# One value product for the high and the low part of the probabilities, in an attention and convolution block

## The chip, the cores and the metric

The kernel runs on one core of a Trainium2 chip. The metric is the device time of one execution in microseconds (us); less is better. The kernel before takes 1517.45 us, the median of three runs (1516.55 to 1518.78).

## The reference

One layer of a streaming encoder on x of 2048 tokens by 1024 features, in float32:

```
h    = rmsnorm(x, norm_g)
q, k, v, z_att, B, C, u, z_conv, g_att, g_conv = split(h @ w_in)
att  = chunked attention(q, k, v), 8 heads of 64, chunks of 64 tokens,
       each sees its own chunk and the 8 before, with a bias by clipped distance
A    = (att * silu(z_att)) @ w_att_out
Bc   = (B * conv3_causal(C * u) * silu(z_conv)) @ w_conv_out
m    = sigmoid(g_att) * A + sigmoid(g_conv) * Bc
out  = rmsnorm(x + m @ w_out, final_norm_g)
```

Inside the attention, per head, the softmax of the scores gives the probabilities p, and the value product is p times v over a band of 576 keys.

## The kernel before

**Number format.** Matrix products are made in a rounded float32 format. To keep float32 accuracy an operand is split into a high part (rounded) and a low part (the rest). A product of two split operands takes three passes (high by high, high by low, low by high; `passes`, lines 137 to 142).

**Stages.** The two halves of the sequence (1024 tokens each) go through the input projection one after the other; the columns of w_in are taken in 24 pairs of tiles, each pair in seven products (a two by two scheme with seven instead of eight). Operands that are used again lie in DRAM (q, k, v, z, gates, weights), and are loaded back. During the second half's projection the attention runs interleaved with it: `attention` is a generator, and the loop over the projection's products calls it so that it comes to its end with them (one step after about every product). Last come the output projections (`half_c`, `half_d`).

**Attention.** The sequence is cut into 4 chunks c of 512 tokens (columns), each with 8 heads h; a chunk and head has 4 units g of 128 queries. Each step of the generator handles three units in different states: the value product of a pair of units, three steps behind (`att_v`, line 223, called for every second unit); the transposes of a unit two steps behind (`att_t`, line 210); the scores of the newest unit (`att_s`, line 186).

- `att_s`: score products into the two-bank tile ps_s (line 195; the tile has one buffer), then VectorE adds the bias and finds the maximum (line 201), ScalarE takes the exponential with the row sum (205), VectorE the reciprocal (206), ScalarE scales (207). The result pr has three buffers.
- `att_t`: TensorE transposes up to five 128x128 blocks of pr into the two-bank tile ps_t (215; one buffer). ScalarE copies them to the high part (220), VectorE writes the rest to the low part (221). High and low part are two tiles, pth and ptl, of 6 key blocks by 256 queries (two units), one buffer each.
- `att_v`: for a pair of units (g0 = 0 or 2) TensorE sums over six key blocks j of 128 keys (line 233). The left operand vv holds, for 128 keys, the high part of v in 64 columns and the low part in 64 others, so the 128 rows of the result are p by v-high and p by v-low. Four blocks are seen by both units (256 columns); block 0 by the first unit alone and block 5 by the second alone (128 columns each). Each block has two matmuls, one with pth and one with ptl, that add up in the same columns. In the first chunk only keys from the sequence's beginning on exist: the spans are fewer.
- Both calls of a head fill one PSUM bank (512 columns, the tile po from a pool of one buffer). After the second call ScalarE copies rows 64 to 127 out (239) and VectorE adds rows 0 to 63 to them (240), into the tile o of a pair of heads (64 rows for each head). After the odd head the pair is multiplied with silu(z) (242), split in high (243) and low (244), and both are stored (246) by DMAs that POOL issues. The tiles zs and o have one buffer each, and so has vv; they are allocated when v of the head is loaded (`load_v`, line 172).

**PSUM.** During the attention: two banks for ps_s, two for ps_t, one for po, three for the projection (ps_d).

**Order of the work.** Except in the first stage, the order in which each engine's queue is filled is not written by hand: a planner in the framework takes the program's order as priority and its own estimate of when each operand is ready, and assigns buffers of a pool as they become free. The engines then work their queues in order. The temporary of the readout (line 238) comes from a pool of eight 128x512 buffers (tag e) that the projection's evictions use as well.

Of the kernel before, what the change touches and what calls it, by code (L numbers as in the profile page):

```python
# [17 lines left out]
P = 128  # L18
# [8 lines left out]
DH = 64  # L27
# [14 lines left out]
def block_kernel(ctx, tc, xb, xt, wp_in, wy, wo, bias, ng, fg, cw, cb, out):  # L42
    nc = tc.nc
# [62 lines left out]
    e = lambda name: ep.tile([P, CH], F32, tag="e", name=name)  # L106
    bank = lambda name: ps_m.tile([P, CH], F32, tag="m", name=name)
# [37 lines left out]
    def attention(ab):  # L145

        at = lambda shape, tag, dt=F32R, bufs=1: ab.tile(shape, dt, tag=tag, name=tag, bufs=bufs)
        pt = [at([P, 6, 2 * P], f"pt{s}") for s in "hl"]
        heads = {}
        values = {}  # L150
        pair = {}
        po = {}
        dma = nc.gpsimd.dma_start

        def load_qk(c, h):
            o = slice(h % 2 * DH, h % 2 * DH + DH)
            q = [at([P, CH], f"q{s}", bufs=2) for s in range(2)]
            kk = at([P, 2 * CH], "kk", bufs=2)
            bs = at([P, WIN], "bs", F32, bufs=2)
            heads[c, h] = (q, kk, bs)  # L160
            for s in range(2):
                for r in (0, DH):
                    dma(q[s][r:r + DH, :].bitcast(F32), q_d[h // 2][s][c][o, :])  # L163
            if c % 2:
                dma(kk.bitcast(F32), k_d[h][c // 2])
            else:
                dma(kk[:, CH:].bitcast(F32), k_d[h][c // 2][:, :CH])
                if c:
                    dma(kk[:, :CH].bitcast(F32), k_d[h][c // 2 - 1][:, CH:])
            dma(bs, bias_d[h])  # L170

        def load_v(c, h):
            vv = at([P, 8, P], "vv")
            values[c, h] = vv
            if c % 2:
                dma(vv.bitcast(F32), v_d[h][c // 2])
            else:
                dma(vv[:, 4:, :].bitcast(F32), v_d[h][c // 2][:, :4, :])
                if c:
                    dma(vv[:, :4, :].bitcast(F32), v_d[h][c // 2 - 1][:, 4:, :])  # L180
            if h % 2 == 0:
                zs = at([P, CH], "zs", F32)
                dma(zs, z_d[h // 2][c])
                pair[c, h // 2] = (zs, at([P, CH], "o", F32))

        def att_s(c, h, g):
            q, kk, bs = heads[c, h]
            nb = 5 if c else g + 1
            n = nb * P
            k1 = CH + (g + 1) * P  # L190
            ps = ps_s.tile([P, 2, CH], F32, tag="s", name="ps_s")
            parts = [(0, n)] if nb < 5 else [(0, WIN // 2), (1, WIN // 2)]
            for i, m in parts:
                for s in range(2):
                    nc.tensor.matmul(ps[:, i, :m], lhsT=q[s][:, g * P:(g + 1) * P], rhs=kk[:, k1 - n + i * m:k1 - n + (i + 1) * m], start=(s == 0), stop=(s == 1))  # L195
            if nb < 5:
                view, bv = ps[:, 0, :n], bs[:, WIN - n:]
            else:
                view, bv = ps[:, :, :WIN // 2], bs.rearrange("p (i m) -> p i m", i=2)
            nmax = small.tile([P, 1], F32, tag="nmax", name="nmax")  # L200
            nc.vector.tensor_tensor_reduce(out=view, in0=view, in1=bv, scale=-0.125, scalar=3.0e38, op0=ALU.add, op1=ALU.min, accum_out=nmax)  # L201
            pr = at([P, WIN], "pr", F32, 3)
            rs = small.tile([P, 1], F32, tag="rs", name="rs")
            out = pr[:, :n] if nb < 5 else pr.rearrange("p (i m) -> p i m", i=2)
            nc.scalar.activation(out, view, AF.Exp, bias=nmax, scale=-1.0, accum_out=rs)  # L205
            nc.vector.reciprocal(rs, rs)  # L206
            nc.scalar.activation(pr[:, :n], pr[:, :n], AF.Identity, scale=rs)  # L207
            return pr, nb

        def att_t(g, pr, nb):  # L210
            hi, lo = pt
            n = nb * P
            ps = ps_t.tile([P, 2 * CH], F32, tag="t", name="ps_t")
            for j in range(nb):
                nc.tensor.transpose(out=ps[:, j * P:(j + 1) * P], in_=pr[:, j * P:(j + 1) * P], identity=ident)  # L215
            o = g % 2
            js = slice(5 - nb + o, 5 + o)
            qs = slice(o * P, (o + 1) * P)
            src = ps[:, :n].rearrange("p (j q) -> p j q", q=P)
            nc.scalar.copy(hi[:, js, qs], src)  # L220
            nc.vector.tensor_sub(lo[:, js, qs], src, hi[:, js, qs].bitcast(F32))  # L221

        def att_v(c, h, g0):

            vv = values[c, h]
            if g0 == 0:
                po[0] = bank("po")
            ps = po[0]
            spans = [(4, 0, 2), (3, 0, 2), (2, 0, 2), (1, 0, 2), (0, 0, 1), (5, 1, 2)]
            js = [s for s in spans if c or g0 + s[0] >= 4]  # L230
            for i, (j, a, b) in enumerate(js):
                for s in pt:
                    nc.tensor.matmul(ps[:, (g0 + a) * P:(g0 + b) * P], lhsT=vv[:, g0 + j, :], rhs=s[:, j, a * P:b * P], start=(i == 0 and s is pt[0]), stop=(i == len(js) - 1 and s is pt[1]))  # L233
            if g0 == 0:
                return
            rows = slice(h % 2 * DH, (h % 2 + 1) * DH)
            zs, o = pair[c, h // 2]
            tmp = e("ot")
            nc.scalar.copy(tmp[rows], ps[DH:P])
            nc.vector.tensor_add(o[rows], ps[0:DH], tmp[rows])  # L240
            if h % 2:
                nc.vector.tensor_mul(o, o, zs)
                nc.scalar.copy(zs.bitcast(F32R), o)
                nc.vector.tensor_sub(o.bitcast(F32R), o, zs)
                for s, t in enumerate((zs, o)):
                    dma(mid_d[0][h // 2][s][c], t)

        todo = [(c, h) for c in range(NC) for h in range(HEADS)]
        units = [(c, h, g) for c, h in todo for g in range(4)]
        held = {}  # L250
        load_qk(*todo[0])
        for i in range(len(units) + BACK):
            u = i - BACK
            if u >= 0 and u % 2:
                att_v(*units[u][:2], units[u][2] - 1)
            if 1 < i < len(units) + 2:
                att_t(units[i - 2][2], *held.pop(i - 2))
            if i < len(units):
                held[i] = att_s(*units[i])
                if i % 4 == 1 and i // 4 + 1 < len(todo):  # L260
                    load_qk(*todo[i // 4 + 1])
                elif i % 4 == 2:
                    load_v(*todo[i // 4])
            yield
# [431 lines left out]
    with tc.manual_schedule(engines=engines):  # L696
# [8 lines left out]
        for q, (p, n, c) in enumerate(plain):  # L705
# [4 lines left out]
            ps = dbank("ps_p")  # L710
# [49 lines left out]
    for s, (p, i) in enumerate(seq):  # L760
# [23 lines left out]
        g0, g1 = 2 * half, 2 * half + 1  # L784
        onto = half == 0 and i in (6, 5, 3)
        if onto:
            ps = uv[p][0]
        elif half == 0 and i in (1, 7):
            ps = (ps_c if i == 1 else ps_h).tile([P, CH], F32, tag="b", name="ps_c")
        else:  # L790
            ps = dbank("ps_d")
# [65 lines left out]
        if n == NPAIR + 1 + PLAIN and i == 3:  # L857
            for _ in mixed:
                pass
            first.close()  # L860
            banks.close()
            ps_s, ps_t, ps_m = (banks.enter_context(tc.tile_pool(name=name, bufs=1, space=PSUM)) for name in ("ps_s", "ps_t", "ps_mm"))
            att = ExitStack()
            ab = attention(att.enter_context(tc.tile_pool(name="ab", bufs=1, side="right")))
            s0 = s
        elif ab:
            while at_stages < (s - s0) * units / (len(seq) - s0 - 1):
                next(ab)
                at_stages += 1
# [333 lines left out]
```

## Time and profile before

| | |
|---|---|
| median of three runs | 1517.45 us |
| the profiled execution | 1515.71 us |
| its span, first to last instruction | 1513.9 us |
| granted TensorE clock, mean | 0.998 |
| value matmuls (line 233), of each part | 336 |
| ... of these 256 columns wide | 224 |
| ... of these 128 columns wide | 112 |
| first and last value matmul | 611.1 and 1175.3 us |
| calls of the readout (lines 239 and 240) | 32 and 32 |
| stores of the tile o (line 246) | 16 |

PE is TensorE's matmul row, PEld its weight loads, which overlap the matmuls; DVE is VectorE, ACT ScalarE, POOL GpSimd, SP SyncE. A row of the timeline has the start, the duration, the engine, the line, the operation with its output and inputs, shapes, and in brackets the idle time ahead of it with what ended it. The matmuls' ends are modelled, so the rate of TensorE is read from starts. A row of the waits has who waited for whom, the total, the number and the longest. Where an instruction waits for several things, the trace names the one that came last.

### The profile page before, as it was taken

Reading aid. Unit: us, or ns where it says so; the run is one execution under the profiler, and the core shown is the slowest. Engines: PE = TensorE matmul, PEld = TensorE weight load, DVE = VectorE, ACT = ScalarE, POOL = GpSimd, SP = SyncE. Lnnn points to the kernel's source line nnn. Section 1 sums busy time; section 2 is a strip of 40 time slices with the busy share of each in tenths; the row PEclk is TensorE's granted clock in tenths of the full one; section 3 lists DMA queues with packets and bytes.
Section 4 is the critical chain, followed back from the end, with each engine's and each line's share of the span. In section 5 each row is a group of like instructions: output and inputs, shape, how many; then the busy total and the mean of one; then the engine's idle time right before and its main releaser. Section 6 shows DMA issues by size and latency. Waiting matters only on the chain. (4 is left out here: it accounts for less than half of the span.)

```text
span 1513.9 us, 21635 instructions
## 1 busy us (share of the span) xinstructions
PE 1484.4 (98%) x7312; PEld 1245.4 (82%) x7312; DVE 1062.4 (70%) x2025; ACT 737.4 (49%) x1367; POOL 163.7 (11%) x310
## 2 busy tenths in 40 slices
PE   9899999999999999999999999999999999999998
PEld 6678888888877788888888888888888788888886
DVE  7977579696557684665666767776755567867687
ACT  7364364444435343555666556666665213423153
POOL 0000000000000002233222222222220000010000
PEclk9999999999999999999999999999999999999999
DMA  5289999989888986999998787877888945877453
GB/s 211 76 283 351 321 366 343 359 299 331 318 295 297 326 314 197 334 345 332 297 302 275 237 260 241 266 257 259 294 271 304 319 126 167 287 250 255 148 166 111
DMA packets 168751, 408.32 MB, mean 270 GB/s; under 512 B 21057, under 2 KB 41537, under 8 KB 168641
## 3 DMA queue, kind: packets, MB, share of 16 engines
q1 hardware_dynamic: 137008, 316.48, 60.7%
q0 software_dynamic: 22272, 73.42, 15.1%
q10 hardware_dynamic: 9360, 17.04, 3.0%
q8 instruction: 58, 0.95, 0.3%
q14 instruction: 53, 0.43, 0.1%
HBM read 251.67 MB, written 155.19 MB: 269 GB/s over the span
## 5 line engine op out<-in xcount | busy, mean ns | idle before, releaser
L205 ACT ACTIVATE pr<-ps_s,nmax 128x640 f32<-128x640 f32 (+4 forms) x128 | 93.3, 729 | 93.8 <-DVE nmax L201 93.1
L163 POOL DMA_DIRECT2D q<-q x128 | 66.7, 526 | 661.3 <-DVE wc L128 582.8
L201 DVE CUSTOM_DVE_ANT_0 ps_s<-ps_s,bs 128x640 f32<-128x640 f32 (+4 forms) x128 | 95.3, 745 | 54.7 <-PE ps_s L195 54.0
L207 ACT ACTIVATE pr<-pr,rs 128x640 f32<-128x640 f32 (+4 forms) x128 | 97.8, 764 | 29.6 <-DVE rs L206 29.2
L128 DVE TENSOR_TENSOR wc<-wraw,wc 128x512 fp32r<-128x512 f32 x120 | 82.2, 687 | 27.7 <-ACT wc L127 27.4
L220 ACT CAST pth<-ps_t 128x640 fp32r<-128x640 f32 (+4 forms) x128 | 79.9, 625 | 43.2 <-PE ps_t L215 42.3
L140 PE MATMUL ps_d<-mid,wy 128*128 128x512 f32 x256 | 99.8, 390 | 0.9 <-ACT wy L127 0.9
L127 ACT CAST wc<-wraw 128x512 fp32r<-128x512 f32 x120 | 74.2, 622 | 53.7 <-PE ps_c L142 26.8
L195 PE MATMUL ps_s<-kk,q 128*128 128x320 f32 (+1 forms) x448 | 97.9, 334 | 2.1 <-ACT pr L205 2.0
L141 PE MATMUL ps_d<-mid,wy 128*128 128x512 f32 x256 | 99.6, 389 | 0.0
L142 PE MATMUL ps_d<-mid,wy 128*128 128x512 f32 x256 | 99.5, 389 | 0.0
L221 DVE TENSOR_TENSOR ptl<-ps_t,pth 128x640 fp32r<-128x640 f32 (+4 forms) x128 | 94.1, 735 | 5.1 <-ACT pth L220 4.7
L215 PE MATMUL ps_t<-ident,pr 128*128 128x128 f32 x560 | 83.9, 276 | 0.3 <-DVE rs L206 0.2
L233 PE MATMUL po<-pth,vv 128*128 128x256 f32 x336 | 78.9, 271 | 2.0 <-DMA vv<-v 2.0
L233 PE MATMUL po<-ptl,vv 128*128 128x256 f32 x336 | 78.2, 281 | 0.0
L195 PEld LDWEIGHTS ps_s<-kk,q 128*128 128x128 f32 x448 | 67.1, 190 | 6.1 <-ACT pr L205 5.7
L1000 PE MATMUL ps_w<-wo,lefth 128*128 128x512 f32 (+1 forms) x240 | 71.9, 382 | 0.0
L215 PEld LDWEIGHTS ps_t<-ident,pr 128*128 128x128 f32 x560 | 63.1, 140 | 10.3 <-issue 2.1
L233 PEld LDWEIGHTS po<-pth,vv 128*128 128x128 f32 x336 | 63.9, 190 | 5.0 <-issue 1.9
L233 PEld LDWEIGHTS po<-ptl,vv 128*128 128x128 f32 x336 | 64.2, 191 | 2.4
L140 PEld LDWEIGHTS ps_d<-mid,wy 128*128 128x128 f32 x256 | 48.0, 188 | 11.6 <-ACT wy L127 1.6
L142 PEld LDWEIGHTS ps_d<-mid,wy 128*128 128x128 f32 x256 | 48.1, 188 | 10.0
(536 smaller groups left out, 4142.0 us busy)
## 6 DMA issues: line engine op xcount, KB each, us to landing
wc<-wc SPq DMA_DIRECT2D x294, 512.0 KB, 5.1
wraw<-wp_in SPq DMA_DIRECT2D x54, 512.0 KB, 5.7
q<-q POOLq DMA_DIRECT2D x128, 128.0 KB, 4.9
gl<-gate SPq DMA_DIRECT2D x64, 256.0 KB, 2.9
mid<-mid SPq DMA_DIRECT2D x64, 256.0 KB, 5.3
wor<-wo SPq DMA_DIRECT2D x56, 256.0 KB, 5.1
bs<-bias POOLq DMA_DIRECT2D x32, 320.0 KB, 7.2
v<-vst SPq DMA_DIRECT2D x64, 128.0 KB, 4.7
```

What stands on the lines that cost most here:

```text
L128: nc.vector.tensor_sub(w[:, 1], src, w[:, 0].bitcast(F32))
L140: nc.tensor.matmul(ps, lhsT=w[:, 0, k, :], rhs=rh[:, cs], start=(first and not onto and k == 0), stop=False, skip_group_check=onto)
L141: nc.tensor.matmul(ps, lhsT=w[:, 0, k, :], rhs=rl[:, cs], start=False, stop=False, skip_group_check=onto)
L142: nc.tensor.matmul(ps, lhsT=w[:, 1, k, :], rhs=rh[:, cs], start=False, stop=(last and k == len(rhs) - 1), skip_group_check=onto)
L195: nc.tensor.matmul(ps[:, i, :m], lhsT=q[s][:, g * P:(g + 1) * P], rhs=kk[:, k1 - n + i * m:k1 - n + (i + 1) * m], start=(s == 0), stop=(s ...
L201: nc.vector.tensor_tensor_reduce(out=view, in0=view, in1=bv, scale=-0.125, scalar=3.0e38, op0=ALU.add, op1=ALU.min, accum_out=nmax)
L205: nc.scalar.activation(out, view, AF.Exp, bias=nmax, scale=-1.0, accum_out=rs)
L207: nc.scalar.activation(pr[:, :n], pr[:, :n], AF.Identity, scale=rs)
L215: nc.tensor.transpose(out=ps[:, j * P:(j + 1) * P], in_=pr[:, j * P:(j + 1) * P], identity=ident)
L220: nc.scalar.copy(hi[:, js, qs], src)
L221: nc.vector.tensor_sub(lo[:, js, qs], src, hi[:, js, qs].bitcast(F32))
L233: nc.tensor.matmul(ps[:, (g0 + a) * P:(g0 + b) * P], lhsT=vv[:, g0 + j, :], rhs=s[:, j, a * P:b * P], start=(i == 0 and s is pt[0]), stop= ...
```

## The change

High and low part get one tile, pt, in which for each key block the 256 columns of the high part stand next to the 256 of the low part. One matmul per key block has both as its right operand, 512 columns wide, or 2 x 128 columns in two runs for the blocks that one unit alone sees. It writes the high part's product to columns 0 to 255 of a bank and the low part's to columns 256 to 511. A bank now holds one pair of units instead of two, so it is taken and read out at each call: ScalarE copies rows 64 to 127 of the high part's columns, VectorE adds rows 0 to 63 of the same columns, and a second add on VectorE joins rows 0 to 63 of the low part's columns and writes to o. The fourth product, v-low by p-low (rows 64 to 127 of the low part's columns), which the kernel before added in, is not read.

```
-        pt = [at([P, 6, 2 * P], f"pt{s}") for s in "hl"]
+        pt = at([P, 6, 2, 2 * P], "pt")
...
         def att_t(g, pr, nb):
-            hi, lo = pt
+            hi, lo = pt[:, :, 0], pt[:, :, 1]
...
         def att_v(c, h, g0):
 
             vv = values[c, h]
-            if g0 == 0:
-                po[0] = bank("po")
-            ps = po[0]
+            ps = bank("po").rearrange("p (s q) -> p s q", s=2)
             spans = [(4, 0, 2), (3, 0, 2), (2, 0, 2), (1, 0, 2), (0, 0, 1), (5, 1, 2)]
             js = [s for s in spans if c or g0 + s[0] >= 4]
             for i, (j, a, b) in enumerate(js):
-                for s in pt:
-                    nc.tensor.matmul(ps[:, (g0 + a) * P:(g0 + b) * P], lhsT=vv[:, g0 + j, :], rhs=s[:, j, a * P:b * P], start=(i == 0 and s is pt[0]), stop=(i == len(js) - 1 and s is pt[1]))
+                nc.tensor.matmul(ps[:, :, a * P:b * P], lhsT=vv[:, g0 + j, :], rhs=pt[:, j, :, a * P:b * P], start=(i == 0), stop=(i == len(js) - 1))
+            rows = slice(h % 2 * DH, (h % 2 + 1) * DH)
+            zs, o = pair[c, h // 2]
+            tmp = e("ot")[rows, :2 * P]
+            nc.scalar.copy(tmp, ps[DH:P, 0])
+            nc.vector.tensor_add(tmp, ps[0:DH, 0], tmp)
+            nc.vector.tensor_add(o[rows, g0 * P:(g0 + 2) * P], ps[0:DH, 1], tmp)
             if g0 == 0:
                 return
-            rows = slice(h % 2 * DH, (h % 2 + 1) * DH)
-            zs, o = pair[c, h // 2]
-            tmp = e("ot")
-            nc.scalar.copy(tmp[rows], ps[DH:P])
-            nc.vector.tensor_add(o[rows], ps[0:DH], tmp[rows])
             if h % 2:
```

More of the change, by code (lines that the diff above doesn't have):

```diff
@@ L151, in attention @@
         pair = {}
-        po = {}
         dma = nc.gpsimd.dma_start
```

## The prediction

> **What bounds the kernel now.** I read the page first, for the share of each engine in the span.
>
> ```profile
> span 1513.9 us, 21635 instructions
> ...
> PE 1484.4 (98%) x7312; PEld 1245.4 (82%) x7312; DVE 1062.4 (70%) x2025; ACT 737.4 (49%) x1367; POOL 163.7 (11%) x310
> ```
>
> TensorE is busy 98% of the span. The change touches only the stretch in which attention runs, so next I read the busy time of each engine between 608 and 1178 us, taken in four windows of which the sum is shown (the first figure is the length, then TensorE, its weight loads, VectorE, ScalarE).
>
> ```profile
> core 0: us, PE busy (x) PEld busy (x) DVE busy (x) ACT busy (x) POOL busy (x), PEclk, DMA share, GB/s
> ...
> sum 570.00, PE 565.56 PEld 491.85 DVE 379.28 ACT 350.12 POOL 145.67; mean PE 141.39 PEld 122.96 DVE 94.82 ACT 87.53 POOL 36.42
> ```
>
> TensorE is idle for 4.4 of 570 us there, VectorE for 191. TensorE's own waits between 600 and 1180 us, longest first (total, times, longest), say the same:
>
> ```profile
> PE po L233 <- DMA vv<-v: 2.0, 2, 1.5
> PE ps_s L195 <- ACT pr L205: 2.0, 6, 0.6
> ```
>
> So this stage is bound by how fast TensorE gets through its instructions, and the change is worth what it takes off that stream, less what it makes TensorE wait. The shown length of a matmul doesn't give that rate, since it overlaps the next one's. I therefore read start against start, in TensorE's timeline around one value product (line 233): the 512-wide matmuls ahead of it, its eight 256-wide ones, its four 128-wide ones, and the transposes behind it.
>
> ```profile
> 799.67 0.39 PE L140 MATMUL ps_d<-t22h,wc 128*128 128x512 f32 x1
> ...
> 801.04 0.28 PE L233 MATMUL po<-pth,vv 128*128 128x256 f32 x1
> ...
> 801.99 0.22 PE L233 MATMUL po<-pth,vv 128*128 128x128 f32 x1
> 802.05 0.28 PE L233 MATMUL po<-ptl,vv 128*128 128x128 f32 x1
> ...
> 802.39 0.73 PE L215 MATMUL ps_t<-ident,pr 128*128 128x128 f32 x5
> ```
>
> Six 512-wide matmuls take 801.04 - 799.67 = 1.37 us, 0.228 each. Eight 256-wide ones take 0.95, 0.119 each. Four 128-wide ones take 0.40, 0.10 each: the first is followed after 0.06, the other three after 0.11 on average. Half the columns of a 256-wide one, at almost its price: each matmul has a weight load of its own, and behind a narrow matmul the load shows. The Trainium skill, "TensorE: Matmul & The Clock Gate", section "LDWEIGHTS (loading the stationary operand)", makes a load as long as its 128 columns at 1.2 GHz, 107 ns; the 0.11 of the trace agrees.
>
> **The change part by part.** *The product.* High and low part of a block stand side by side, so one matmul streams both against one load of vv. Two 256-wide matmuls become one 512-wide one; two 128-wide ones become one of 256 columns, read and written as two runs of 128. The counts, one row for each width (the other part has the same):
>
> ```profile
> L233 PE MATMUL po<-pth,vv 128*128 128x256 f32 x224 | 56.6, 284 | 2.0 <-DMA vv<-v 2.0
> ...
> L233 PE MATMUL po<-ptl,vv 128*128 128x128 f32 x112 | 28.4, 277 | 0.0
> ```
>
> A full span goes from 2 x 0.119 to 0.228: 0.010 saved, 224 times, 2.1 us. A half span goes from 2 x 0.10 to one matmul of 256 columns. No row shows one in two runs. From below it is bounded by the 0.10 of a load, from above by the 0.228 of a 512-wide matmul; I take the 0.119 of the same number of columns in one run, the nearest row. That saves 0.08, 112 times, 9.0 us. Together 11.1 us come off TensorE (13.2 at the lower bound; 2.1 - 112 x 0.028 = -1.0 at the upper).
>
> The Trainium skill has a rule against this: "PSUM — Partial Sum Buffer", section "Specifications (TRN2)", says that any access pattern that isn't contiguous slows matmuls significantly. No row here shows such a pattern, and the page gives no price; the upper bound above stands in for it.
>
> *The reading out.* Before, ScalarE copies and VectorE adds 512 columns once per head. After, each of two calls per head has a copy of 256 columns and two adds of 256. The durations, of the readout itself and of the nearest 256-wide operations that read PSUM (nanoseconds, least/median/most):
>
> ```profile
> L239 ACT COPY ot<-po x32: 580/582/586, 620.3 to 1176.1; 64x512 f32<-64x512 f32 x32
> L240 DVE TENSOR_TENSOR o<-po,ot x32: 675/683/685, 620.9 to 1176.7; 64x512 f32<-64x512 f32 x32
> ```
>
> ```profile
> L457 ACT CAST vst<-vt x32: 346/372/394, 422.6 to 774.0; 128x256 fp32r<-128x256 f32 x32
> L458 DVE TENSOR_TENSOR vst<-vt,vst x32: 402/420/428, 423.0 to 774.4; 128x256 fp32r<-128x256 f32 x32
> ```
>
> ScalarE: 2 x 0.37 - 0.58 = +0.16 us per head, 5 us over 32 heads. VectorE: 4 x 0.42 - 0.68 = +1.0 us per head, 32 us in all; of that 0.84 falls behind the first call, where nothing stood before, and 0.16 behind the second. VectorE goes from 379 to about 411 us of the 570 and stays far from being the bound. But its queue is in order: behind the adds stand the score reduction (line 201), which through the exponential (line 205) frees the only score bank, and the low-part subtraction (line 221), which frees the only transpose bank. What is tight there now, from the rows of the score product:
>
> ```profile
>   ACT pr L205: 7.7, 17
> ```
>
> Seventeen of the 128 score products find their bank released last by the exponential. Half of all steps get adds, so some 8 tight ones do, by 0.84 or 0.16, 0.50 on average: 4 us if nothing takes it up, 0 if VectorE's idle third always does. I take 2. The product's own bank, now taken once per call, is read right behind the call, and the next call begins some 9 us later (801.04, and the row of 811.63 below, which ends the next one).
>
> *A new wait.* The tile o has one buffer. Before, a pair's first write to it came with the pair's second call; now it comes with the first call, by the second add. That add must wait until the store of the pair before (line 246) has read o, and on VectorE line 201 queues behind it. One change of pair, in the timeline:
>
> ```profile
> 807.44 0.54 POOL L246 DMA_DIRECT2D mid<-o  x1 [0.18 <-issue]
> ...
> 811.63 0.27 PE L233 MATMUL po<-ptl,vv 128*128 128x128 f32 x1
> ...
> 813.10 0.83 DVE L201 CUSTOM_DVE_ANT_0 ps_s<-ps_s,bs 128x640 f32<-128x640 f32 x1 [1.82 <-PE ps_s L195]
> ...
> 814.02 0.80 ACT L205 ACTIVATE pr<-ps_s,nmax 128x640 f32<-128x640 f32 x1 [0.82 <-DVE nmax L201]
> ...
> 816.12 0.83 PE L195 MATMUL ps_s<-kk,q 128*128 128x320 f32 x4
> ```
>
> ```profile
> DMA to landing us min/median/max: 3.6/5.2/6.4
> ```
>
> The store lands at 807.44 + 5.2 = 812.6. The product ends at 811.9, 0.2 earlier after the change; with copy, first add and the hand-overs between them (estimate 0.2) the second add is ready at 811.7 + 0.37 + 0.42 + 0.2 = 812.7: no wait at the median, 1.1 us for the slowest store. Line 201 would then start 1.2 late, and the cover is 816.12 - 814.82 = 1.3: nothing lost. Where the store is issued late there is no cover:
>
> ```profile
> 1072.72 0.54 POOL L246 DMA_DIRECT2D mid<-o  x1 [3.12 <-DVE rs L206]
> ...
> 1075.64 0.82 DVE L201 CUSTOM_DVE_ANT_0 ps_s<-ps_s,bs 128x640 f32<-128x640 f32 x1
> ...
> 1078.47 0.83 PE L195 MATMUL ps_s<-kk,q 128*128 128x320 f32 x4
> ```
>
> It would land at 1077.9, the add end at 1078.3, line 201 start 2.7 late; of the 2.83 to the next score product the chain needs 814.82 - 813.10 = 1.7, which leaves 1.1 of cover: 1.6 us lost. There are 15 changes of pair. I take two such, 3.2 us; the bounds are none and all 15, 24 us. The planner that orders the queues could also put line 201 ahead of the add, which is the lower bound.
>
> The store itself, the loads of vv and z on POOL's queue, and SP's queue keep their places; stores move with o, by a few tenths.
>
> **Sum.** 11.1 - 2.0 - 3.2 = 5.9 us. The profiled execution took 1515.71 (span 1513.9 and 1.8 around it), 1.7 under the median of the runs, 1517.45; it becomes 1509.8, and the median 1511.5.
>
> **The rivals.** *The readout eats the gain.* The adds come late on VectorE more often than I count: if a quarter of the 32 added us shows on TensorE (8 us), and the store still costs 1, 11.1 - 8 - 1 leaves 2 us, about 1515. Against it: VectorE idles 191 us of the stage; for it: those 17 tight places. Chance 0.14.
>
> *Slower: the store holds VectorE at each change of pair.* If POOL issues it late every time, 15 x 1.6 = 24 us, and 11.1 - 2 - 24 gives 1532. It decides from 9.1 / 15 = 0.6 us of TensorE per change. For it: the median landing and the add are within 0.1 us of each other. Against: the 1.3 of cover. Chance 0.09.
>
> *Slower: two runs cost double.* The half spans at 0.228 make the product 1.0 slower; with the waits 1517.45 + 1.0 + 5.2 = 1523.7. This is where the PSUM page's rule would lead. Against: the runs are 128 long. Chance 0.05.
>
> *Only columns count.* If the 0.06 after the first 128-wide matmul were its price, four would cost 0.24 against 2 x 0.119, and full spans gain next to nothing: no gain, the waits remain, 1522.7. Here the change would not do what it says. Against: the three 0.11 right behind. The Trainium skill, the TensorE page again, section "Back-to-back issue gap", has such a formula for a matmul alone, columns over 2.4 GHz plus 2.5 ns; by it six fewer matmuls save 15 ns per call; the 0.11 contradicts it. Chance 0.02.
>
> **How the numbers follow.** The forecast has 0.70. The range runs from 1506 (all of 11.1, no waits: 1506.3) to 1520: the first rival lies inside, and of the second the part up to 0.75 us per change (1517.45 - 11.1 + 2 + 11.3 = 1519.7). The forecast's own range is 1506 to 1514. A measurement of this kernel can tell 0.2%, 3 us, from no change: faster 0.70, same 0.14, slower 0.09 + 0.05 + 0.02 = 0.16.
>
> **What would show it.** In the timeline: 512-wide value products 0.228 apart, two-run ones 0.12, a full product 1.15 instead of 1.35 us; 336 value matmuls. VectorE's total up by 32 us. In the waits: VectorE's second add on the store of o, at most 15 times; TensorE's waits on line 205 up by a few us. I am wrong in the sum if two-run matmuls show 0.2 apart, in the waits if TensorE's idle time in the stage grows by over 8 us.

## The result, and the profile after

The changed kernel takes 1505.36 us, the median of four runs (1500.44 to 1508.27); the kernel before, on the same chip, 1518.12 (four runs). The ratio is 0.9915, 95% interval 0.9887 to 0.9943: faster by 12.8 us, where 5.9 were forecast. Timed again in five runs (first experiment below) the changed kernel came to 1504.38 and the kernel before to 1517.27, ratio 0.9918 (0.9903 to 0.9934).

The page after, its span and its line of busy times:

```profile
span 1506.5 us, 21077 instructions
## 1 busy us (share of the span) xinstructions
PE 1475.3 (98%) x6976; PEld 1226.2 (81%) x6976; DVE 1090.5 (72%) x2121; ACT 740.1 (49%) x1399; POOL 163.8 (11%) x310
```

TensorE is still busy 98% of the span, with 7312 - 6976 = 336 matmuls fewer. VectorE has 28 us more.

TensorE's timeline around one full product, six matmuls merged in a row:

```profile
795.37 1.30 PE L229 MATMUL po<-pt,vv 128*128 128x512 f32 x6
796.52 0.71 PE L214 MATMUL ps_t<-ident,pr 128*128 128x128 f32 x5
```

The same stretch, asked for from 796.4 us on, so that the row begins with the fourth matmul:

```profile
796.05 0.62 PE L229 MATMUL po<-pt,vv 128*128 128x512 f32 x3
```

The product takes 796.52 - 795.37 = 1.15 us, where it took 1.35. Three 512-wide matmuls take 0.68, 0.227 each; the fourth and the two in two runs take 0.47, so the two take about 0.12 each. Two runs of 128 cost what one run of 256 does. The rule of the Trainium skill, "PSUM — Partial Sum Buffer", section "Specifications (TRN2)", that the prediction set against this did not show here.

The readout, by tile (nanoseconds, least/median/most; below the dots who held up these instructions, in total and how often):

```profile
L233 ACT COPY ot<-po x64: 367/369/373, 615.2 to 1168.8; 64x256 f32<-64x256 f32 x64
L234 DVE TENSOR_TENSOR ot<-po,ot x64: 406/417/419, 615.8 to 1169.2; 64x256 f32<-64x256 f32 x64
L235 DVE TENSOR_TENSOR o<-po,ot x64: 403/417/421, 616.2 to 1169.6; 64x256 f32<-64x256 f32 x64
...
  DMA mid<-o: 4.4, 5
```

The durations are those that the forecast took from other lines. The new wait is there, at 5 of the 15 changes of pair, 4.4 us in all on VectorE. TensorE's waits between 600 and 1180 us:

```profile
PE po L229 <- DMA vv<-v: 3.2, 2, 1.8
PE po L229 <- DVE w L825: 0.8, 1, 0.8
PE ps_d L140 <- ACT wy L127: 0.8, 1, 0.8
PE ps_s L194 <- ACT pr L204: 0.5, 1, 0.5
```

They come to 5.3 us, where the rows of the same view before come to 5.1, and the two longest are for vv, which the change doesn't touch. The waits for the score bank show more fully in the row of the line of the score products:

```profile
  ACT pr L204: 5.2, 14
```

Before, this row had 7.7 us in 17 places. The row adds up the idle time ahead of the weight loads and ahead of the matmuls of the line, so a place where both wait counts twice. The weight loads alone, before and after (the last figure is what the exponential ended):

```profile
L195 PEld LDWEIGHTS ps_s<-kk,q 128*128 128x128 f32 x448 | 67.1, 190 | 6.1 <-ACT pr L205 5.7
...
L194 PEld LDWEIGHTS ps_s<-kk,q 128*128 128x128 f32 x448 | 67.6, 190 | 5.6 <-ACT pr L204 4.8
```

They waited 5.7 us in 11 places before and 4.8 in 13 after; in the profile of e1, another execution of the changed kernel, 5.5 in 14. So the waits did not grow, and the price that the forecast put on the readout is not there. The timeline shows how it was avoided:

```profile
796.98 0.83 PE L194 MATMUL ps_s<-kk,q 128*128 128x320 f32 x4
...
797.85 0.83 DVE L200 CUSTOM_DVE_ANT_0 ps_s<-ps_s,bs 128x640 f32<-128x640 f32 x1 [0.20 <-PE ps_s L194]
...
798.77 0.42 DVE L234 TENSOR_TENSOR ot<-po,ot 64x256 f32<-64x256 f32 x1
...
800.08 0.42 DVE L235 TENSOR_TENSOR o<-po,ot 64x256 f32<-64x256 f32 x1
```

The product ends at 796.5, and both adds belong to it. Yet the score reduction (now line 200) of the scores that began after it stands ahead of them on VectorE. The planner put 30 of the 64 second adds, and 16 of the first ones, behind the reduction of the next scores (counted in the trace: starts of lines 235 and 234 against line 200, behind each product). In the kernel before, 6 of the 32 adds stood behind it.

The profiled execution of the changed kernel is the slowest of its four, and part of that is a stretch of 3.4 us at half clock inside the attention (last section), which the profile of e1 doesn't have.

### The profile page after: what moved, and what is told of

It reads as the page before. It is cut to its first block, busy times and chain, and to the rows that moved or that the text cites. A ratio compares the mean times of both kernels' runs of the same rounds, so it can differ in the third digit from the quotient of the medians.

```text
span 1506.5 us, 21077 instructions
## 1 busy us (share of the span) xinstructions
PE 1475.3 (98%) x6976; PEld 1226.2 (81%) x6976; DVE 1090.5 (72%) x2121; ACT 740.1 (49%) x1399; POOL 163.8 (11%) x310
## 5 line engine op out<-in xcount | busy, mean ns | idle before, releaser
L220 DVE TENSOR_TENSOR pt<-ps_t,pt 128x640 fp32r<-128x640 f32 (+4 forms) x128 | 94.1, 735 | 3.4 <-ACT pt L219 2.5
L219 ACT CAST pt<-ps_t 128x640 fp32r<-128x640 f32 (+4 forms) x128 | 80.1, 626 | 21.9 <-PE ps_t L214 20.7
L229 PE MATMUL po<-pt,vv 128*128 128x512 f32 x336 | 75.5, 356 | 4.1 <-DMA vv<-v 3.2
L229 PEld LDWEIGHTS po<-pt,vv 128*128 128x128 f32 x336 | 62.1, 188 | 19.1 <-issue 3.5
L140 PEld LDWEIGHTS ps_d<-mid,wy 128*128 128x128 f32 x256 | 48.0, 188 | 11.1 <-ACT wy L127 1.2
L234 DVE TENSOR_TENSOR ot<-po,ot 64x256 f32<-64x256 f32 x64 | 26.6, 415 | 41.3 <-ACT ot L233 40.4
L141 PEld LDWEIGHTS ps_d<-mid,wy 128*128 128x128 f32 x256 | 48.0, 188 | 10.1
L142 PEld LDWEIGHTS ps_d<-mid,wy 128*128 128x128 f32 x256 | 48.1, 188 | 9.9
```

Of the source, the lines that this page charges most:

```text
L140: nc.tensor.matmul(ps, lhsT=w[:, 0, k, :], rhs=rh[:, cs], start=(first and not onto and k == 0), stop=False, skip_group_check=onto)
L141: nc.tensor.matmul(ps, lhsT=w[:, 0, k, :], rhs=rl[:, cs], start=False, stop=False, skip_group_check=onto)
L142: nc.tensor.matmul(ps, lhsT=w[:, 1, k, :], rhs=rh[:, cs], start=False, stop=(last and k == len(rhs) - 1), skip_group_check=onto)
L229: nc.tensor.matmul(ps[:, :, a * P:b * P], lhsT=vv[:, g0 + j, :], rhs=pt[:, j, :, a * P:b * P], start=(i == 0), stop=(i == len(js) - 1))
```

## The experiments

All kernels were timed in five rounds beside the kernel before, whose median in the four sets of runs was 1517.08 to 1517.48 us. The sets (e1 to e4, e5 to e8, e9 to e12, e13 to e15) ran on four chips, so kernels of different sets are best compared by their ratios to before.

**The change again, and its parts.** Theory A: the exposed weight loads go, and the rest is free. Theory B: the forecast's sum.

e1 is the changed kernel itself.

> The changed kernel as it is, timed again beside the others. Theory A (the narrow matmuls' exposed weight loads go, 11.1 us, and VectorE's and ScalarE's added work and the new wait cost nothing): 11 us under before. Theory B (the forecast: 11.1 less 5.2 of waits): 6 us under before. If single executions differ by several us, A puts that down to half-clock windows of 3.4 us, each worth about 1.7 us, in the profile's clock.

Measured 1504.38 (1502.56 to 1507.84), ratio 0.9918 (0.9903 to 0.9934): 12.9 under before. A is nearer. The two profiled executions of this kernel (1508.27 and 1503.04 us) differ by the one half-clock stretch of the last section, which explains 1.7 of the 5.2 us between them; the rest is not worked out.

e2 has the readout without the merged product:

```
-                nc.tensor.matmul(ps[:, :, a * P:b * P], lhsT=vv[:, g0 + j, :], rhs=pt[:, j, :, a * P:b * P], start=(i == 0), stop=...)
+                for s in range(2):
+                    nc.tensor.matmul(ps[:, s, a * P:b * P], lhsT=vv[:, g0 + j, :], rhs=pt[:, j, s, a * P:b * P], start=(i == s == 0), stop=...)
```

> The new layout, banks and readout per call, but two matmuls per key block as before (672 value matmuls, high and low part into their own columns). Theory A: the readout is free, within 1.5 us of before. Theory B: 5 us slower than before. A third, C (the other order that the planner makes of it is worth something by itself): 2 us or more faster than before.

Measured 1520.36, ratio 1.0021 (1.0005 to 1.0036): 3.1 slower, between A and B. Here the readout does cost, and the scores' wait for their bank shows it:

```profile
  ACT pr L204: 10.6, 23
```

10.6 us in 23 places, against 7.7 in 17 before (weight loads alone: 8.0 in 16 against 5.7 in 11). Only 12 of the 64 second adds stand behind the reduction in this kernel. That is what the next set of experiments takes up.

e3 and e4 merge one sort of span each:

```
+                for ss in ((slice(0, 2),) if b - a == 2 else (slice(0, 1), slice(1, 2))):     # e3; e4 has b - a == 1
+                    nc.tensor.matmul(ps[:, ss, a * P:b * P], lhsT=vv[:, g0 + j, :], rhs=pt[:, j, ss, a * P:b * P], ...)
```

> As the changed kernel, but only the key blocks that both units see are merged into 512-wide matmuls (224 of them); the 112 half spans keep two 128-wide matmuls each. Theory A: 2 us under before. Theory B: 3 us above before. In the timeline four 512-wide ones at 0.228 us, then four 128-wide ones in 0.40 us.

Measured 1517.25, ratio 1.0002 (0.9992 to 1.0013).

> The complement: only the 112 half spans are merged, into matmuls of two runs of 128 columns; the full spans keep two 256-wide matmuls each. Theory A: 9 us under before, at 0.12 us per two-run matmul. Theory B: 4 us under before. If two runs cost more than one (the page's rule), the two-run matmuls stand 0.2 us apart and the kernel is no faster than before.

Measured 1510.46, ratio 0.9955 (0.9939 to 0.9970). Against e2, which has the same readout, the full spans are worth 3.1 us and the half spans 9.9; 2.1 and 9.0 were forecast. The gain lies where the narrow matmuls were. Against before, neither A nor B gets all three of e2 to e4 right. From e2 the parts add up to 13.0, and the whole is 16.0; the twelve runs of e4 lie between 1505.72 and 1516.61, so these 3 us are not clear of noise. What differs visibly between the kernels is the planner's order: it put 12, 16, 29 and 30 of the second adds behind the reduction in e2, e3, e4 and e1. Theory D says that this matters: the place of the adds on VectorE relative to the score reduction sets what the readout costs. Its rival E: VectorE has room, and the place is no matter.

**The place of the adds.** e5 is the changed kernel with the reduction of the step queued behind both adds, at all calls (an edge of order alone, no wait):

```
+            lastadd.append(nc.vector.tensor_add(o[rows, g0 * P:(g0 + 2) * P], ps[0:DH, 1], tmp))
...
+            with tc.issue_after(lastadd.pop().ins) if lastadd else ExitStack():
                 nc.vector.tensor_tensor_reduce(out=view, ...)
```

> The changed kernel, with the score reduction of the same step queued behind both adds at all 64 calls (in the changed kernel the planner put 30 of the 64 second adds behind it, in the kernel with the readout alone 12). Theory D (what the readout costs is set by how often the adds stand ahead of the score reduction): 3 us or more slower than the changed kernel, about 1508. Theory E (the place of the adds is no matter, VectorE has room either way): the same as the changed kernel within 1.5 us, about 1504.5.

Measured 1510.24 (1508.17 to 1512.67), ratio 0.9952 (0.9938 to 0.9967): 5.9 slower than e1. This is the order that the forecast assumed throughout, and the time is within 1.3 us of the forecast's. One call in it:

```profile
804.37 0.83 PE L195 MATMUL ps_s<-kk,q 128*128 128x320 f32 x4
...
805.07 0.42 DVE L236 TENSOR_TENSOR ot<-po,ot 64x256 f32<-64x256 f32 x1
805.52 0.82 DVE L222 TENSOR_TENSOR pt<-ps_t,pt 128x640 fp32r<-128x640 f32 x1
806.38 0.42 DVE L237 TENSOR_TENSOR o<-po,ot 64x256 f32<-64x256 f32 x1
806.83 0.83 DVE L202 CUSTOM_DVE_ANT_0 ps_s<-ps_s,bs 128x640 f32<-128x640 f32 x1
...
807.80 0.79 ACT L206 ACTIVATE pr<-ps_s,nmax 128x640 f32<-128x640 f32 x1 [2.37 <-DVE nmax L202]
...
808.73 0.59 PEld L195 LDWEIGHTS ps_s<-kk,q 128*128 128x128 f32 x4 [0.47 <-ACT pr L206]
808.73 0.85 PE L195 MATMUL ps_s<-kk,q 128*128 128x320 f32 x4 [0.23 <-ACT pr L206]
```

The scores of 804.37 end at 805.2. Their reduction (line 202 here) starts at 806.83, behind two adds and a subtraction; the exponential ends at 808.6, and the next scores start right then, with a wait: their weight loads waited for it. Over the kernel the row of the score bank has

```profile
  ACT pr L206: 13.8, 36
```

e6 is the opposite: the copy and the adds are issued behind `att_s` of the same step, and the adds queue behind its reduction.

```
+                read = att_v(*units[u][:2], units[u][2] - 1)       # the product alone
...
                 held[i] = att_s(*units[i])
...
+            if u >= 0 and u % 2:
+                att_o(*read)                                       # copy, adds, and the pair's end
...
+            with tc.issue_after(red[0].ins):
                 nc.vector.tensor_add(tmp, ps[0:DH, 0], tmp)
                 nc.vector.tensor_add(o[rows, g0 * P:(g0 + 2) * P], ps[0:DH, 1], tmp)
```

> The changed kernel, with the copy and the adds put behind the scores of the same step in the program, and the adds queued behind the score reduction at all calls. D: 1 to 3 us faster than the changed kernel, about 1502. E: the same within 1.5 us.

Measured 1501.07 (1500.11 to 1502.25), ratio 0.9892 (0.9877 to 0.9907): 9.2 under e5 with the same instructions. On ScalarE, 7 of the 64 copies moved behind the exponential of the same step (none stood there in e5), so nearly all that differs is VectorE's order. Its row of the score bank:

```profile
  ACT pr L205: 3.2, 8
```

D stands, E falls. From adds first (e5) over the planner's own order (e1) to adds last (e6) the weight loads alone wait 11.9 us in 30 places, 5.5 in 14, 3.2 in 8, and the time is 1510.2, 1504.4, 1501.1.

e7 does the same to e2 (two narrow matmuls, new readout, adds last).

> The readout alone (two narrow matmuls per key block as before), with the adds behind the score reduction at all calls. D: the 3 us that the readout alone cost are gone, within 1 us of the kernel before. E: they stay, 3 us slower than before.

Measured 1515.45, ratio 0.9984 (0.9976 to 0.9993): the 3 us are gone, and 1.6 more, a little beyond what D expected.

e15 applies it to the kernel before, whose readout has one add of 512 columns per head; the edit is that of e6.

> The kernel before, with its one add of 512 columns queued behind the score reduction at all 32 readouts. Its waits ahead of scores and transposes were about 5 us: if the order is worth it there too, 2 to 4 us faster than before, 1514; if its one add per head is no trouble, the same within 1 us.

Measured 1513.09, ratio 0.9973 (0.9962 to 0.9984): 4.4 faster, and the row of the score bank is nearly empty.

```profile
  ACT pr L206: 0.9, 3
```

So part of what e6 gains isn't the change's. With the adds behind the reduction in both, the change is worth 1513.09 - 1501.07 = 12.0 us (11.6 when each is taken against the kernel before of its own set). D does not say that the new readout is then free: e7, which has it and the same order as e15, gained 1.6 us on before where e15 gained 4.4. The intervals just overlap, so a price of up to some 3 us may remain.

e8 asks how much work VectorE takes before TensorE notices: the second add is done three times (`for _ in range(3):`, the same values each time).

> The changed kernel with the second add done three times over (the same result each time): 128 more adds of 0.417 us, 53 us more on VectorE, 1.67 us for each call's adds in place of 0.83. If VectorE's idle time takes it up: within 3 us of the changed kernel. If a third of the added time shows on TensorE (the forecast's share for tight places, doubled): 15 us or more slower.

Measured 1532.63, ratio 1.0099 (1.0082 to 1.0116): 28 us slower than e1 for 53 us of adds. TensorE's longest waits, and the busy times between 608 and 1190 us:

```profile
PE ps_t L214 <- DVE pt L220: 8.8, 6, 3.0
PE po L229 <- DVE pt L220: 4.6, 2, 2.9
PE ps_s L194 <- ACT pr L204: 3.7, 6, 1.0
```

```profile
sum 582.00, PE 559.64 PEld 468.82 DVE 451.84 ACT 349.95 POOL 145.99; mean PE 559.64 PEld 468.82 DVE 451.84 ACT 349.95 POOL 145.99
```

VectorE is busy 78% of that stretch, far from full, and already holds TensorE at the transposes' bank, at the products (whose low part it writes) and at the score bank. But the 28 us are not the price of VectorE's own work alone. Its wait for the store of o grew as well, to 25.4 us, where e1 has 6.6 in 5 places:

```profile
DVE o L236 <- DMA mid<-o: 25.4, 12, 4.3
```

And this profile has three half-clock stretches in the attention, 1.7 us each, where e1 has none.

**The store wait.** e9 is e5 with two buffers for o. The room for it comes from giving the gate tiles of the last stage two pools (two buffers early, three after the attention) instead of one of five. e13 is the control with the two pools alone. The order of adds, reductions and subtractions on VectorE is the same in e5, e9 and e13.

```
-                pair[c, h // 2] = (zs, at([P, CH], "o", F32))
+                pair[c, h // 2] = (zs, at([P, CH], "o", F32, 2))
...
-            gp = pool("gp", 5)
+            gp = [pool("gp", 2)]                       # and after the attention: gp.append(pool("gpb", 3))
```

> The kernel with the adds first (1510.2 us), with a second buffer for the tile o, so that no add waits for the store of the pair before; the room comes from giving the gate tiles of the last stage two pools in place of one. The planner's order of adds, reductions and subtractions on VectorE is the same. If the store wait is a main part of what adds ahead cost (the forecast's 3.2 us): 1507 or less. If the adds' own time in front of the reduction is the cost: 1510 within 1 us.

> The kernel with the adds first, with the two pools for the gate tiles but one buffer for o: the control of the run with two buffers for o. If the 3.6 us there were the store wait: as the kernel with the adds first, 1510. If they came with the pools: 1506.6.

Measured 1506.62, ratio 0.9930 (0.9917 to 0.9944), for e9 and 1509.37, ratio 0.9953 (0.9936 to 0.9970), for the control: 2.8 us by the medians, though the intervals overlap. In the control VectorE waits for the store 7 times:

```profile
DVE o L237 <- DMA mid<-o: 3.6, 7, 1.5
```

So with the adds ahead, the store wait costs by the medians about what the forecast took, 3.2; the overlap leaves its size open. e14 gives the changed kernel two buffers for o:

> The changed kernel with two buffers for o (and the two pools). If the store wait costs the changed kernel what the forecast took: 3 us faster, 1501.5. If the planner's order, with half of the second adds behind the reduction, already covers it: within 1 us, 1504.5.

Measured 1503.96, ratio 0.9913 (0.9900 to 0.9925), the same as e1: in the planner's order the store wait costs nothing that can be told.

**Two buffers for vv.** TensorE's longest waits after the change were for vv, so e10, e11 and e12 give vv two buffers (`bufs=2`, room as in e9), in the changed kernel, in e6 and in the kernel before.

> The changed kernel with a second buffer for vv, loaded while the head before still uses the first (room as in the run before). TensorE's waits for vv, 1 to 3 us in two or three places, and any half-clock window behind them go: 2 to 5 us faster than the changed kernel, 1500 to 1502, and single executions closer together. If the waits only move to another operand: the same, 1504.5.

Measured 1504.76, ratio 0.9918 (0.9903 to 0.9932): no gain. The wait for vv is gone from the profile, and another has its place:

```profile
PE ps_t L214 <- DVE pt L220: 3.0, 3, 2.1
```

> Adds behind the reduction and two buffers for vv together: 1497 to 1499 if the two effects add, 1501 if the wait for vv was already covered there.

Measured 1499.44 (1498.86 to 1499.80), ratio 0.9884 (0.9871 to 0.9898), the fastest kernel of the study: 17.7 under before, 1.6 under e6, which the intervals don't separate.

> The kernel before with two buffers for vv, the control of the two runs above: 2 us faster than before (its waits for vv were 2.0 us in the profile), 1515. If the second buffer is worth 5 us or more here too, it and not the change explains part of what the changed kernel gains.

Measured 1514.83, ratio 0.9985 (0.9976 to 0.9994): 2.3 faster, as its waits for vv said.

## Why the prediction was right or wrong

*What bounds the stage, and the product.* Right. TensorE's stream was the bound; full spans at 0.227, two-run ones at 0.12, 1.15 us per product. Summed over the trace, from the start of each value matmul to the next start, the products take 75.6 us before and 65.3 in e1. The transposes behind a product, from start to start inside their group, go from 24.1 to 22.7 (24.0 in e3, which keeps the 128-wide matmuls, and 22.6 in e4, which merges them): the narrow matmuls' weight loads had also held up the transposes behind them, which the forecast did not count (the five behind a product shown in the prediction last 0.73, after the change 0.71). Together 11.7, where 11.1 was forecast; e6 against e15 gives 12.0.

*The readout's durations.* Right: 0.37 and 0.42 us. The readout's own rows on VectorE rose by 31.4 us (two of 26.6 against one of 21.8), where 32 were forecast; VectorE's total rose by 28.

*The adds ahead of the reduction, and the new wait.* This is the step that failed: "behind the adds stand the score reduction ... and the low-part subtraction". It took the order of the program for the order on VectorE at every call. The forecast named the planner's other order as the lower bound of the store wait alone, and gave it no weight. The planner put 30 of the 64 second adds behind the reduction. The two terms that it led to, 2.0 for the readout and 3.2 for the store, are what made the forecast too small. With the assumed order forced (e5) the kernel takes 1510.2, where the forecast had 1511.5. In the planner's own order nothing of the 5.2 us is seen: 11.7 us came off TensorE's stream and 12.8 were measured, and the weight loads' waits for the score bank stand at 4.8 to 5.5 us against 5.7 before, where the forecast had them grow. Whether the 1 us more than the stream gave is a gain of the order isn't shown; it is within the noise of four runs. e15 shows that the better order was open to the kernel before, too. The forecast's reading of the score bank's row was off as well: its 17 tight places were 11, of which 6 counted twice. That alone would have made the term of 2.0 smaller, not removed it.

*The store wait.* The mechanism was right: VectorE's second add waits for the store, at 5 of at most 15 places. Its price of 3.2 us fits with the adds first (about 2.8, intervals overlapping) and not in the changed kernel (e14). That the size fits is partly luck: the forecast took two changes of pair at 1.6 us, and in the control VectorE waits at seven, 3.6 us in all.

*The rivals.* None came true. That the readout eats the gain was closest: e2 shows that it costs 3.1 us by itself in the planner's order. Of two runs at double price and of columns alone there is no trace.

*The range* did not hold the time: its lower end, 1506, was set at the full product gain with no added waits at all, and the measured median lies 0.6 below. The forecast had taken the best case for the edge, and the kernel came out at the best case.

What stays open: e3, e4 and e1 don't add up from e2 (13.0 against 16.0). In the traces the products and the transposes behind them do add up, within half a microsecond: 2.2 us less than e2 in e3, 9.1 in e4, 11.8 in e1. So what doesn't add up is noise or lies in TensorE's waits. The count of second adds behind the reduction (12, 16, 29, 30 in e2, e3, e4, e1) doesn't explain it, since e4 and e1 have nearly the same. Open too is what the new readout costs with the adds last (e7 against e15).

## What to carry to other kernels

Where TensorE is the bound, read start against start by width: a matmul whose columns take less time than its weight load pays for the load, and putting two such side by side behind one load saves nearly a whole matmul (here 0.20 us for two became 0.12). What an operation added to an engine with idle time costs depends on what it stands ahead of in that engine's queue, and not on its duration alone: look for the instruction there that frees a single buffer, and put the new work behind it by hand. Where a planner orders the queues, cost an edit in both orders, and take neither for granted.

## What the runs showed of the hardware

A wait of TensorE of about 2 us can be followed by a stretch at half clock, and a longer one can be without. In the profile of the changed kernel, TensorE waits for vv until 720.03 and soon after runs 512-wide matmuls 0.43 apart instead of 0.228:

```profile
720.03 0.59 PE L229 MATMUL po<-pt,vv 128*128 128x512 f32 x2 [1.84 <-DMA vv<-v]
...
721.68 0.63 PE L140 MATMUL ps_d<-t50h,wc 128*128 128x512 f32 x1
...
722.11 0.63 PE L141 MATMUL ps_d<-t50l,wc 128*128 128x512 f32 x1
```

The busy times of that stretch, with the granted clock as the third column from the end:

```profile
720.90:724.40 3.50, 3.50 (x12) 2.93 (x11) 2.31 (x5) 1.43 (x4) 0.00 (x0) 0.51 0.98 370
```

The clock is 0.51 for 3.5 us, so 1.7 us are lost on top of the wait. It came once in the attention of this profile, and not in that of e1. The profile of e14 has the same at the same load: a wait of 2.40 us for vv until 718.22, then a clock of 0.51 from 718.9 to 722.4. In e7 a wait of 3.15 us until 509.54, ahead of the attention, was followed by full clock (1.00 from 509 to 516). No run here shows what decides it. The Trainium skill, "TensorE: Matmul & The Clock Gate", Part 1, has the gate drop to half after an idle window of about 3.4 us; here a wait of 1.84 us stood ahead of it.
